# The last layer norm's second tile: two pieces of 256 columns for one of 512, and the piece in SBUF finished by GpSimd

## The chip, the cores and the metric

The kernel runs on one core of a Trainium2 chip. A core has TensorE (PE: matmuls, its weight loads shown apart as PEld), VectorE (DVE), ScalarE (ACT), GpSimd (POOL) and SyncE (SP, which only issues DMAs here). Data lies in SBUF and in PSUM, both of 128 partitions; matmuls write PSUM. The metric is the device time of one execution in microseconds, the median over the runs; lower is better.

## The reference

The program is a decoder trunk of two layers over 256 tokens of 1024 numbers, all in float32. A layer is a feed-forward half-step, a mixer (a gated spatial unit beside differential attention) and a second feed-forward half-step, each followed by a residual and a layer norm:

```
h = _swiglu(x, ffn_w1[l, 1], ffn_w3[l, 1], ffn_w2[l, 1])
x = _layernorm(ALPHA * x + 0.5 * h, ln_g[l, 2], ln_b[l, 2])
```

with `_layernorm(x, g, b) = (x - mean) * rsqrt(var + eps) * g + b`, mean and variance taken over the 1024 numbers of a token. The norm behind the second layer's second feed-forward is the last work of the program; its result is the output. The change lies in that norm.

## The kernel before, in words

Weights stream in from HBM, and each is split into a high and a low part in a faster matmul format; a product is three matmuls (high by high, low by high, high by low) that add up in PSUM. TensorE's order is the order in which the code is written. The other engines' order comes from a planner that sorts by priority and by dependences between regions of tiles; a wait is put in wherever an engine needs another's result. PSUM is given out as two groups of four banks, `bank()` and `side_bank()`, each handed out again when its last reader is done.

The 256 tokens are two tiles `t` of 128 (one token for each partition). The last feed-forward's second product, `gemm_seven`, makes 512 columns of the output at a time. Its last stretch goes over the second half of the output columns: for tile 0 all of 512:1024, then for tile 1 first 512:768 and then 768:1024 (line 410 is the matmul there and in the loops around it). Whenever a group of columns is done, `Norm.part` adds it to the residual in `y` (L625) and takes statistics of 256 columns each (L629). In tile 1 of the last norm, all columns below 768 are also multiplied at once by `g` (L631), since mean and variance of the row aren't known yet. So the work behind the last matmul concerns mostly the columns 768:1024 and the whole row's statistics.

`Norm.finish` then ends the tile. In the last norm:

- L636 (VectorE) joins the statistics to mean and variance, `mv`.
- L660 (GpSimd) adds eps to the variance, L661 (ScalarE) takes the square root; L674 to L676 (VectorE) make of these the factor `r` of each token, with one correction step.
- For tile 1 the pieces 512:768 and 0:512 of the row are taken through TensorE: an identity matmul (L666) copies `y * g` into PSUM, and a matmul with a diagonal matrix that holds minus the mean (made by ScalarE, L668) adds `-mean * g` to it (L670). A float32 matmul is two passes, each with its own weight load. The two pieces lie in two side banks.
- The third piece, 768:1024, stays in SBUF: L672 (VectorE) makes `(y - mean) * g` of it in one instruction.
- L678 (VectorE) multiplies each piece by `r` and adds `b`, in one scalar-tensor-tensor instruction; L679 stores it to HBM from the queues of SP and ScalarE (ACT) in turns. The pieces go in the order 768:1024 (SP), 512:768 (ACT), 0:512 (SP).

Tile 0 has the same three pieces, but all stay in SBUF and on VectorE; it ends while TensorE still works on tile 1.

Of the kernel before, what the change touches and what calls it, by code (L numbers as in the profile page):

```python
# [17 lines left out]
ALU = mybir.AluOpType  # L18
# [3 lines left out]
D = 1024  # L22
T = 256
NT = T // P
# [30 lines left out]
def trunk(ctx, tc, x, xT, w13a, w13b, w2, wb, wqk, wu, wg, wgr, wbr, wbrr, wo, gateb, gatebr, sgug, sgub, sguwT, sgubias, lam, diffg,  # L55
          lng, lnb, lngT, lnbT, cosT, sinT, out):
    nc = tc.nc
    V, A, G, PE = nc.vector, nc.scalar, nc.gpsimd, nc.tensor
# [22 lines left out]
    def side_bank():  # L81
        return psum.tile([P, 512], F32, tag="side", name=name("sbank"))
# [15 lines left out]
    def t512(s, n=3):  # L98
        return tmp.tile([P, 512], F32, tag="main", name=name(s), bufs=n)

    def s512(s, n=4):
        return tmp.tile([P, 512], F32, tag="side", name=name(s), bufs=n)

    def sm(s, n, dtype=F32, bufs=2):
        return small.tile([P, n], dtype, tag=f"{s}{n}", name=name(s), bufs=bufs)
# [31 lines left out]
    def beside(task, delay):  # L137
        tasks.append([clock[0] + delay, task])
# [16 lines left out]
    def behind(ins):  # L155

        return tc.issue_after(ins) if ins is not None else nullcontext()
# [93 lines left out]
    def rsqrt(v, eps):  # L251


        ve, y = sm("ve", 1), sm("yi", 1, I32)
        V.tensor_scalar(out=ve, in0=v, scalar1=eps, scalar2=None, op0=ALU.add)
        V.tensor_scalar(out=y, in0=ve.bitcast(I32), scalar1=-0.5, scalar2=RSQRT_START, op0=ALU.mult, op1=ALU.add)
        y = y.bitcast(F32)
        for e in (-26 / 27, -8 / 9, -2 / 3):
            a, z = sm("nwa", 1), sm("nwy", 1)
            V.tensor_scalar(out=a, in0=y, scalar1=y, scalar2=ve, op0=ALU.mult, op1=ALU.mult)  # L260
            V.tensor_scalar(out=z, in0=a, scalar1=3.0 * 2.0 ** e, scalar2=y, op0=ALU.subtract, op1=ALU.mult)
            y = z
        return y
# [321 lines left out]
    class Norm:  # L585
# [47 lines left out]
        def finish(self, t, waits):  # L633
            y = self.y[t]
            mv = sm("mv", 2)
            V.bn_aggr(out=mv, in_=self.st[t])  # L636
            if not self.last:
                r = rsqrt(mv[:, 1:2], self.eps)
                halves = slice(0, 512), slice(512, D)
                if t:  # L640
                    self.via += [t512("nvia") for _ in halves]
                for h in (0, 1) if t else (1, 0):
                    s = halves[h]
                    with behind(self.ends[t]):
                        self.ends[t] = V.tensor_scalar(out=y[:, s], in0=y[:, s], scalar1=mv[:, 0:1], scalar2=r,
                                                       op0=ALU.subtract, op1=ALU.mult).ins
                    if t:
                        self.ends[t] = self.plane(V, t, h, 1)
                if t == 0:
                    self.via.append(s512("nvia"))  # L650
                    for w in range(2):
                        self.ends[t] = self.plane(V, 0, 1, w)
                    beside(self.turned(waits), 0)
                else:
                    beside(self.sent(), 1.2)
                    beside(self.tokens(1), 10.8)
                return
            cuts = [slice(*c) for c in ((768, D), (512, 768), (0, 512))]
            ve, sd, r, a = (sm(n, 1) for n in ("ve", "nwy", "nwa", "nwy"))
            G.tensor_scalar(out=ve, in0=mv[:, 1:2], scalar1=self.eps, scalar2=None, op0=ALU.add)  # L660
            A.activation(sd, mv[:, 1:2], AF.Sqrt, bias=self.eps_t)  # L661
            rows = [y[:, s] for s in cuts]
            if t == NT - 1:
                rows[1:] = [side_bank()[:, : s.stop - s.start] for s in cuts[1:]]
                for b, s in zip(rows[1:], cuts[1:]):
                    PE.matmul(b, ident, y[:, s], start=True, stop=False)  # L666
                diag = self.minus[:, P : 2 * P]
                A.activation(diag, self.minus[:, :P], AF.Copy, scale=mv[:, 0:1])  # L668
                for b, s in zip(rows[1:], cuts[1:]):
                    PE.matmul(b, diag, self.g[:, s], start=False, stop=True)  # L670
            for s in cuts[: 1 if t == NT - 1 else 3]:
                V.scalar_tensor_tensor(out=y[:, s], in0=y[:, s], scalar=mv[:, 0:1], in1=self.g[:, s],  # L672
                                       op0=ALU.subtract, op1=ALU.mult)
            V.reciprocal(out=r, in_=sd)  # L674
            V.tensor_scalar(out=a, in0=r, scalar1=r, scalar2=ve, op0=ALU.mult, op1=ALU.mult)
            V.tensor_scalar(out=r, in0=a, scalar1=3.0, scalar2=r, op0=ALU.subtract, op1=ALU.mult)  # L676
            for n, (s, v) in enumerate(zip(cuts, rows)):
                V.scalar_tensor_tensor(out=y[:, s], in0=v, scalar=r, in1=self.b[:, s], op0=ALU.mult, op1=ALU.add)  # L678
                (nc.sync, A)[n % 2].dma_start(out[t * P : (t + 1) * P, s], y[:, s])  # L679

        def plane(self, eng, t, h, w):
# [653 lines left out]
```

## Time and profile before

| | |
|---|---|
| median of 3 runs | 1187.51 us (1187.22 to 1187.51) |
| profiled execution | 1188.13 us, span 1186.4 us |
| TensorE busy | 1180.8 us (100% of the span) |
| VectorE / ScalarE / GpSimd busy | 85% / 70% / 24% |
| GpSimd instructions | 352 |
| granted TensorE clock | 1.000 |

The span runs from the first to the last instruction of the core; the device time of the same execution has 1.7 us more around it. In the views, a row of the timeline is the start, the duration, engine, line, operation, output and inputs, shapes and the number of instructions merged into it; in brackets stands how long the engine was idle before and what ended that. A matmul's duration holds its way through the array, so that durations of matmuls in sequence overlap. Rows of one line give the durations' minimum, median and maximum.

### The profile page before, as it was taken

How to read it: one execution, taken by the hardware profiler on the slowest of the kernel's cores; microseconds unless marked ns; L12 is line 12 of the kernel's file. 1: busy time of each engine (PE TensorE's matmuls, PEld its weight loads, DVE VectorE, ACT ScalarE, POOL GpSimd, SP SyncE). 2: the span in 40 equal slices, each digit the busy share in tenths (PEclk: the TensorE clock that was granted, in tenths of full speed). 3: DMA queues.
4: the chain of work that ended last, by engine and by line, in shares of the span. 5: the costliest groups of instructions: out<-in, count | busy, mean ns of one | idle time of the engine just before them, and what ended most of it. 6: DMA issues, size and time to landing. Idle time of an engine off the chain costs nothing.

```text
span 1186.4 us, 16662 instructions
## 1 busy us (share of the span) xinstructions
PE 1180.8 (100%) x5771; PEld 994.4 (84%) x5771; DVE 1011.4 (85%) x1558; ACT 828.8 (70%) x1418; POOL 286.3 (24%) x352
## 2 busy tenths in 40 slices
PE   9999999999999999999999999999999999999998
PEld 8888888888888888888888888888888888888887
DVE  6989989788688989889899889888965989988895
ACT  6688658559955677886567876576788556679761
POOL 1011301247420220071020171004564112102300
PEclk9999999999999999999999999999999999999999
DMA  9868976768865658689668699586666755786881
GB/s 354 258 206 258 291 268 209 265 196 235 248 203 174 228 186 275 187 275 271 235 222 262 193 274 283 195 293 231 215 203 204 257 181 167 252 254 210 272 252 36
DMA packets 129476, 275.10 MB, mean 232 GB/s; under 512 B 89024, under 2 KB 90096, under 8 KB 105328
## 3 DMA queue, kind: packets, MB, share of 16 engines
q1 hardware_dynamic: 121968, 248.80, 63.1%
q0 software_dynamic: 6992, 24.71, 8.7%
q8 instruction: 45, 0.74, 0.2%
q10 hardware_dynamic: 432, 0.52, 0.1%
q14 instruction: 39, 0.32, 0.1%
HBM read 248.05 MB, written 1.05 MB: 210 GB/s over the span
## 4 chain that ended last, share of the span: by engine, by line
PE 99%; DMA 0%; DVE 0%; ACT 0%; issue 0%; ACTq 0%
PE bank L283 46%; PE bank L295 15%; PE sbank L376 12%; PE bank L410 10%; PE bank L302 8%; PE sbank L410 3%; PE bank L521 2%; PE sbank L994 1%; PE bank L376 1%; PE sbank L1050 1%; PE sbank L1168 1%; PE sbank L1048 0%; DMA xtok<-in_xT 0%; PE sbank L691 0%; PE sbank L670 0%; DVE xtok L678 0%
## 5 line engine op out<-in xcount | busy, mean ns | idle before, releaser
L197 DVE TENSOR_TENSOR wlo<-raw,whi 128x1024 fp32r<-128x1024 f32 (+1 forms) x346 | 378.7, 1121 | 53.1 <-ACT whi L195 39.2
L195 ACT ACTIVATE whi<-raw 128x1024 fp32r<-128x1024 f32 (+1 forms) x350 | 323.7, 952 | 136.5 <-PE bank L283 43.1
L283 PE MATMUL bank<-whi,x 128*128 128x512 f32 x1224 | 386.1, 390 | 0.0
L283 PEld LDWEIGHTS bank<-whi,x 128*128 128x128 f32 x1224 | 229.8, 188 | 47.5
L283 PE MATMUL bank<-wlo,x 128*128 128x512 f32 x612 | 238.2, 389 | 0.0
L249 DVE TENSOR_TENSOR wlo<-raw,whi 128x1024 fp32r<-128x1024 f32 (+1 forms) x124 | 143.7, 1182 | 18.1 <-ACT whi L247 9.4
L247 ACT ACTIVATE whi<-raw 128x1024 fp32r<-128x1024 f32 (+1 forms) x124 | 121.7, 1000 | 49.1 <-DVE raw L359 24.5
L295 PE MATMUL bank<-x,whi 128*128 128x512 f32 x640 | 153.3, 391 | 0.0
L295 PEld LDWEIGHTS bank<-x,whi 128*128 128x128 f32 x640 | 118.2, 188 | 23.8
L283 PEld LDWEIGHTS bank<-wlo,x 128*128 128x128 f32 x612 | 114.9, 188 | 23.4
L229 POOL COPY seven<-seven 128x512 uint16<-128x512 uint16 x16 | 58.1, 3690 | 134.4 <-DMA seven<-seven 74.0
L302 PEld LDWEIGHTS bank<-x,wlo 128*128 128x128 f32 x640 | 81.4, 191 | 2.9
L302 PE MATMUL bank<-x,wlo 128*128 128x256 f32 x640 | 82.6, 283 | 0.0
L410 PE MATMUL bank<-whi,hhi 128*128 128x512 f32 (+1 forms) x182 | 68.2, 374 | 0.0
L410 PE MATMUL bank<-whi,hlo 128*128 128x512 f32 (+1 forms) x182 | 67.9, 373 | 0.0
L410 PE MATMUL bank<-wlo,hhi 128*128 128x512 f32 (+1 forms) x182 | 67.9, 373 | 0.0
L970 POOL TENSOR_TENSOR swap<-swap,sin_t 128x512 f32<-128x512 f32 x16 | 27.8, 1737 | 101.2 <-DMA swap<-z 75.7
L734 POOL COPY nvia<-ntwo 128x256 uint16<-128x256 uint16 x20 | 9.9, 541 | 162.3 <-DMA ntwo<-nvia 150.0
L303 ACT ACTIVATE r<-bank 128x256 f32<-128x256 f32 x96 | 34.9, 372 | 16.5 <-PE bank L302 16.4
L376 PE MATMUL sbank<-whi,xhs 128*128 128x512 f32 x128 | 42.0, 389 | 0.0
L359 DVE TENSOR_TENSOR raw<-raw,home 128x1024 f32<-128x1024 f32 x32 | 38.5, 1217 | 1.2 <-DMA home<-in_w13b 1.2
L410 PEld LDWEIGHTS bank<-whi,hlo 128*128 128x128 f32 x182 | 34.3, 188 | 6.1
(283 smaller groups left out, 2148.7 us busy)
## 6 DMA issues: line engine op xcount, KB each, us to landing
raw<-in_w13b SPq DMA_DIRECT2D x68, 1024.0 KB, 5.8
raw<-in_w SPq DMA_DIRECT2D x32, 1024.0 KB, 6.9
raw<-in_wb SPq DMA_DIRECT2D x16, 1024.0 KB, 6.0
raw<-in_wqk SPq DMA_DIRECT2D x16, 1024.0 KB, 6.2
home<-in_w13b SPq DMA_DIRECT2D x16, 512.0 KB, 6.1
raw<-in_w13a SPq DMA_DIRECT2D x8, 1024.0 KB, 4.9
home<-in_w SPq DMA_DIRECT2D x16, 512.0 KB, 4.6
raw<-in_wgr SPq DMA_DIRECT2D x8, 1024.0 KB, 5.3
```

What stands on the lines that cost most here:

```text
L195: inline(A, A.activation(h, r, AF.Copy).ins)
L197: low = eng.tensor_tensor(out=w, in0=r, in1=h.bitcast(F32), op=ALU.subtract).ins
L229: eng.tensor_copy(out=o, in_=i)
L247: a = A.activation(hi, src, AF.Copy).ins
L249: return a, eng.tensor_tensor(out=lo, in0=src, in1=hi.bitcast(F32), op=ALU.subtract).ins
L283: PE.matmul(ps, xx, w, start=start and n == 0, stop=stop and n == 2)
L295: PE.matmul(b[-1], hi[:, k * P : (k + 1) * P], xc(k), start=k == 0, stop=False)
L302: PE.matmul(b[n][:, :T], lo[:, k * P : (k + 1) * P], xc(k)[:, :T], start=False, stop=k == KT - 1)
L303: emptied[0] = A.activation(r[:, s], b[n][:, T:], AF.Copy, scale=scale).ins
L359: inline(V, V.tensor_tensor(out=v, in0=v, in1=m, op=ALU.add).ins)
L376: PE.matmul(ps, x[o](k), y, start=start and k == n == 0, stop=stop and k == 3 and n == 2, skip_group_check=True)
L410: PE.matmul(q[c][t][:, :n] if o == 0 else more[:, :n], x(k, t), y, start=k == 8 and m == 0 and (c, t) != (1, 0), stop=k == FT - 1 and m == ...
```

## The change

For tile 1 of the last norm, and only there:

- The piece 0:512 is cut into 256:512 and 0:256. With 512:768 that makes three pieces of 256 columns in PSUM, in three side banks, with three identity and three diagonal matmuls instead of two each.
- The last step of the piece in SBUF (768:1024) goes from VectorE's one instruction to two on GpSimd: a multiply by `r` and an add of `b`, both in place.
- The order of the last step is now 512:768, 256:512, 0:256 (VectorE) and then 768:1024 (GpSimd). There are four stores instead of three, in turns on SP, ACT, SP, ACT.

Tile 0, the other norms and everything ahead of the last norm are written as before.

```
-            cuts = [slice(*c) for c in ((768, D), (512, 768), (0, 512))]
+            end = t == NT - 1
+            cuts = [slice(*c) for c in ((768, D), (512, 768), *(((256, 512), (0, 256)) if end else ((0, 512),)))]
             ve, sd, r, a = (sm(n, 1) for n in ("ve", "nwy", "nwa", "nwy"))
...
-            if t == NT - 1:
+            if end:
                 rows[1:] = [side_bank()[:, : s.stop - s.start] for s in cuts[1:]]
                 for b, s in zip(rows[1:], cuts[1:]):
                     PE.matmul(b, ident, y[:, s], start=True, stop=False)
...
-            for s in cuts[: 1 if t == NT - 1 else 3]:
+            for s in cuts[: 1 if end else 3]:
                 V.scalar_tensor_tensor(out=y[:, s], in0=y[:, s], scalar=mv[:, 0:1], in1=self.g[:, s],
                                        op0=ALU.subtract, op1=ALU.mult)
...
-            for n, (s, v) in enumerate(zip(cuts, rows)):
-                V.scalar_tensor_tensor(out=y[:, s], in0=v, scalar=r, in1=self.b[:, s], op0=ALU.mult, op1=ALU.add)
+            each = list(zip(cuts, rows))
+            for n, (s, v) in enumerate(each[1:] + each[:1] if end else each):
+                if end and s.stop == D:
+                    G.tensor_scalar(out=v, in0=v, scalar1=r, scalar2=None, op0=ALU.mult)
+                    G.tensor_tensor(out=v, in0=v, in1=self.b[:, s], op=ALU.add)
+                else:
+                    V.scalar_tensor_tensor(out=y[:, s], in0=v, scalar=r, in1=self.b[:, s], op0=ALU.mult, op1=ALU.add)
                 (nc.sync, A)[n % 2].dma_start(out[t * P : (t + 1) * P, s], y[:, s])
```

## The prediction

> **What bounds the kernel now.** I read the page first: the span, the busy shares and the chain that ended last.
>
> ```profile
> span 1186.4 us, 16662 instructions
> PE 1180.8 (100%) x5771; PEld 994.4 (84%) x5771; DVE 1011.4 (85%) x1558; ACT 828.8 (70%) x1418; POOL 286.3 (24%) x352
> PE 99%; DMA 0%; DVE 0%; ACT 0%; issue 0%; ACTq 0%
> ```
>
> TensorE carries 99% of the chain. The change touches nothing before the last norm, so only the tail behind the last matmuls of the feed-forward can move. That tail is the chain from the end of those matmuls (1179.16 us) to the end of the span, some 7.3 us, and I read it in order of time. From the chain of waits:
>
> ```profile
> 1180.10 0.27 DVE mv L636
> 1180.46 0.29 ACT nwy L661
> 1180.75 0.30 ACT minus L668
> 1181.10 1.57 PE sbank L670 x4
> 1182.69 0.75 DVE xtok L678
> ```
>
> Mean and variance go to ScalarE, which makes the diagonal matrix; TensorE adds the summand with the mean in four passes until 1182.67; VectorE then makes the last 512 columns. The timeline of VectorE and of the queues (start, duration) has the rest:
>
> ```profile
> 1181.40 0.22 DVE L676 TENSOR_SCALAR nwa<-nwy,nwa 128x1 f32<-128x1 f32 x1
> 1181.65 0.48 DVE L678 SCALAR_TENSOR_TENSOR xtok<-xtok,nwa,bc 128x256 f32<-128x256 f32 x1
> 1182.05 0.48 DVE L678 SCALAR_TENSOR_TENSOR xtok<-sbank,nwa,bc 128x256 f32<-128x256 f32 x1
> 1182.69 0.75 DVE L678 SCALAR_TENSOR_TENSOR xtok<-sbank,nwa,bc 128x512 f32<-128x512 f32 x1 [0.16 <-PE sbank L670]
> 1182.56 0.34 ACTq L679 DMA_DIRECT2D out_x<-xtok  x1
> 1183.47 0.33 SPq L679 DMA_DIRECT2D out_x<-xtok  x1
> ...
> out_x<-xtok SPq DMA_DIRECT2D x1, 256.0 KB, 2.0
> out_x<-xtok SPq DMA_DIRECT2D x1, 128.0 KB, 1.7
> out_x<-xtok ACTq DMA_DIRECT2D x1, 128.0 KB, 1.7
> ```
>
> The factor r is ready at 1181.62 (L676). The last piece is written at 1183.44, its store is issued at 1183.47 and lands 2.0 later, at 1185.47; what is left to 1186.4 is the program's closing and does not depend on the change. The last three rows are the DMA view's, with KB and us from issue to landing. So the end is set by: diagonal ready, TensorE's passes, one VectorE instruction of 0.75, one store of 2.0.
>
> **The change part by part.**
>
> *TensorE: two pieces become three.* Both the identity matmuls (L666) and the diagonal ones (L670) go from a 256 and a 512 to three of 256, each in two passes: four more passes in all, and as many weight loads.
>
> ```profile
> 1178.98 0.59 PE L666 MATMUL sbank<-xtok,ident 128*128 128x256 f32 x2
> 1179.41 1.02 PE L666 MATMUL sbank<-xtok,ident 128*128 128x512 f32 x2
> L666 PE MATMUL sbank<-xtok,ident 128*128 128x512 f32 x2 | 1.0, 593 | 0.0
> L666 PE MATMUL sbank<-xtok,ident 128*128 128x256 f32 x2 | 0.6, 378 | 0.0
> 1181.10 0.70 PE L670 MATMUL sbank<-bc,minus 128*128 128x256 f32 x2 [0.66 <-ACT minus L668]
> 1181.63 1.02 PE L670 MATMUL sbank<-bc,minus 128*128 128x512 f32 x2
> 1181.10 0.73 PEld L670 LDWEIGHTS sbank<-bc,minus 128*128 128x128 f32 x4 [1.49 <-ACT minus L668]
> ```
>
> Two 256-column passes span 0.59 with 0.378 each, so a pass starts 0.21 after the one before; for 512 columns it is 1.02 - 0.593 = 0.43, twice that. Cutting therefore costs no streaming, as long as the weight load (0.73 for four, below 0.19 each) fits into 0.21. The diagonal passes end for 512:768 at 1181.80 (1181.10 + 0.70), for 256:512 at 1181.80 + 0.42 = 1182.22, for 0:256 at 1182.65: the same end as before, 1182.67. Bound: the first two L670 passes stand 0.70 - 0.38 = 0.32 apart; at that spacing for the two added passes the end is 0.2 later. Below nothing there is no gain, since the columns are the same. I take zero, because L666's passes in sequence are the nearest rows. The identity passes are hidden in the 0.66 us in which TensorE waits for the diagonal; without that cover they too would cost at most 0.2.
>
> *The third PSUM bank.* The tag has four buffers; the norm takes the two not held by the second product and, now, one that this stage had used:
>
> ```profile
> 1169.11 0.69 DVE L625 SCALAR_TENSOR_TENSOR xtok<-xtok,sbank 128x512 f32<-128x512 f32 x1 [5.73 <-PE sbank L410]
> ```
>
> Its last reader ended at 1169.80, 9 us before L666, so the wait costs nothing. If the bank still were held, every later pass would stand behind it.
>
> *VectorE.* The SBUF piece leaves, so 512:768 is first. It can start at 1181.80 plus the 0.03 of a wait (r is there at 1181.65 already), and instructions in a row follow at 0.40 (1181.65 to 1182.05). 256:512 starts at about 1182.25, 0:256 at 1182.69 as before, when its passes are done; it takes 0.48 for 0.75 and ends at 1183.17. Gain 0.27. L672, which centres the SBUF piece, stays on VectorE.
>
> *GpSimd.* The piece 768:1024 gets two new instructions, a multiply by a column and an add of a 128x256 f32 tile. No row shows the first. Rows of one line, minimum/median/maximum ns:
>
> ```profile
> L249 POOL TENSOR_TENSOR x<-nvia,x x10: 732/737/752, 182.8 to 1006.9; 128x256 fp32r<-128x256 f32 x10
> L734 POOL COPY nvia<-ntwo x20: 470/480/1049, 179.5 to 1013.9; 128x256 uint16<-128x256 uint16 x20
> L275 POOL TENSOR_SCALAR nwa<-nwa x24: 220/224/1290, 270.6 to 915.3; 128x4 f32<-128x4 f32 x24
> L970 POOL TENSOR_TENSOR swap<-swap,sin_t x16: 1287/1703/2842, 216.2 to 845.0; 128x512 f32<-128x512 f32 x16
> 1180.45 0.21 POOL L660 TENSOR_SCALAR ve<-mv 128x1 f32<-128x1 f32 x1 [8.96 <-DVE mv L636]
> ```
>
> The add is L249's form: 0.74. The multiply lies between 0.22 (L275, four columns) and 0.74 (two inputs of that size); I take the one-input copy of 256 columns, 0.48. GpSimd started L660 0.08 after mv (1180.37), so here it starts at 1181.70, ends the multiply at 1182.18, the add, with 0.1 between, at 1183.02. With both at 0.74 it is 1183.28. The upper end is a stretched one: L970 went from 1.29 to 2.84, a factor of 2.2, which gives 1.06 + 0.1 + 1.63, until 1184.5. Nothing waits for GpSimd but this piece's store.
>
> Is it stretched? Two moments when GpSimd and VectorE worked together:
>
> ```profile
> 233.47 1.29 POOL L970 TENSOR_TENSOR swap<-swap,sin_t 128x512 f32<-128x512 f32 x1 [4.57 <-ACT pp L1008]
> 234.02 0.42 DVE L307 SCALAR_TENSOR_TENSOR z<-bank,r 128x256 f32<-128x256 f32 x1 [0.95 <-ACT r L303]
> 801.19 1.29 POOL L970 TENSOR_TENSOR swap<-swap,sin_t 128x512 f32<-128x512 f32 x1 [22.73 <-DMA swap<-z]
> 801.55 2.01 DVE L197 TENSOR_TENSOR wlo<-raw,whi 128x1024 fp32r<-128x1024 f32 x1
> ```
>
> Beside the scalar-tensor-tensor that reads PSUM and one SBUF tile both kept their undisturbed times (1.29, L970's minimum; 0.42). Beside the subtraction with two SBUF inputs VectorE paid instead: L197 took 2.01. The three L678 beside the new GpSimd work read PSUM and one SBUF tile, so I take no stretch. The Trainium skill, "SBUF — State Buffer", section "SBUF: two separate sides", says that GpSimd shares one port pair with VectorE under an exclusive lock, taken by a VectorE instruction with two SBUF inputs; by that rule the L678 from PSUM take no lock, and the two rows agree.
>
> The same skill's "GPSIMD Engine Reference", section "Engine selection", speaks against the change: it wants elementwise work on VectorE, GpSimd being about half as fast on two inputs. Weighed in this kernel: left on VectorE, the piece adds one slot of 0.40 and 0:256 starts at 1182.85, not 1182.69, so the rule costs 0.16 as long as GpSimd is not last; by the sum above it is not.
>
> *Queues.* Three stores become four, all of 128 KB. SP issues 512:768 (about 1182.35), then 0:256 at 1183.20; ACT's queue issues 256:512 at about 1182.78 (VectorE's end 1182.73, and 0.03), and behind it 768:1024, not before 0.38 later, at 1183.16; GpSimd's 1183.02 is hidden by that. So the last two stores go out within 0.05 of each other and share the DMA engines:
>
> ```profile
> 1182.95:1183.90 0.95, 0.00 (x0) 0.00 (x0) 0.49 (x1) 0.00 (x0) 0.00 (x0) 1.00 0.79 276
> 1184.30:1185.02 0.72, 0.00 (x0) 0.00 (x0) 0.00 (x0) 0.00 (x0) 0.00 (x0) 1.00 0.94 364
> ```
>
> These are two stretches of the span (length; last column GB/s): the two 128 KB stores together, and the 256 KB one. Alone, 128 KB lands in 1.7: 1183.20 + 1.7 = 1184.90, a gain of 0.57. Behind the other 128 KB at 364 GB/s, 0.36 later: 1185.26, a gain of 0.21. At 276 GB/s (0.47), with 0.1 for what is left of the 256:512 store: 1185.47, nothing. I take the middle, since the sharing is certain and the pieces' packets come back to back.
>
> *Sum.* VectorE -0.27, the smaller last store -0.30 (2.0 to 1.7), its neighbour +0.36: -0.21 us. The profiled execution took 1188.13 (span 1186.4 and 1.7 around it), so 1187.9 against it; it stands 0.6 above the median of the runs shown, 1187.51. Against the median: **1187.3 us**.
>
> **The rivals.**
>
> *No gain.* The stores overlap at 276 GB/s, or the added weight loads cost their 0.2: the end moves by less than 0.1 and the time is 1187.5. For it: the row with 276. Against: that stretch holds two stores issued 0.40 apart, with a dip between them.
>
> *GpSimd and VectorE block each other* (slower). If the L678 and the GpSimd instructions exclude each other, they go in turns from 1181.70: multiply to 1182.18, first L678 to 1182.66, add to 1183.40, two more L678 to 1184.36; the last store goes at 1184.39 and lands at 1186.09, +0.62 us, so 1188.1. Stretched by 2.2 instead, GpSimd ends at 1184.5 and its store lands at 1186.2, +0.8, so 1188.3. It decides from the point where GpSimd ends after about 1183.7 (1183.75 + 1.7 = 1185.45), some 2.0 us for the two instructions. For it: L970's maximum; against: the row at 233.47.
>
> *Slower by over 0.2%.* That is 2.4 us: GpSimd would have to end near 1186.1, 4.4 us after r. Only a multiply by a column that costs 3.6 us would do it. The costliest group of GpSimd has such a mean, but for copies of 512 columns that overlap work with two SBUF inputs:
>
> ```profile
> L229 POOL COPY seven<-seven 128x512 uint16<-128x512 uint16 x16 | 58.1, 3690 | 134.4 <-DMA seven<-seven 74.0
> ```
>
> **How the numbers follow.** A change of 0.2%, 2.4 us, is about what a measurement of this kernel can tell from no change. Chances: forecast 0.62, no gain 0.18, blocking 0.14, slower by over 0.2% 0.04, some effect that shortens by as much, which no row supports, 0.02. Only the last two leave the band: faster 0.02, same 0.94, slower 0.04. The likeliest case's own range is 1186.9 to 1187.8 (gain 0.57 to 0, and 0.3 of scatter, as among the runs shown). To hold 8 in 10 the range takes in the blocking and, below, the largest gain with the scatter doubled: 1186.5 to 1188.3.
>
> **What would show it.** Right: six L670 passes that end within 0.05 of 1.57 after the diagonal; three L678 from PSUM of 0.48, the last starting at the end of the passes; GpSimd with some 0.48 and 0.74, done before ACT's queue has issued 256:512; the last two stores within 0.1 of each other, landing about 0.2 earlier. Wrong: GpSimd's rows over 1 us, an L678 that starts late without TensorE as its releaser, L670 passes 0.3 apart, or a store of 768:1024 that lands last by more than 0.2. A time out of the range would mean that something before 1179 us moved, which I hold the change not to touch.

## The result and the profile after

The changed kernel takes 1190.2 us (median of 15 runs, 1189.76 to 1191.37), the kernel before 1187.51 (15 runs, 1187.21 to 1188.39): a ratio of 1.0022, with a 95% interval of 1.0015 to 1.0029. That is 2.7 us more, where the prediction had 0.2 less. In all that follows, differences in us are between medians; the ratios are taken over the single runs and so aren't exactly the quotients of the medians.

The head of the page of the changed kernel:

```profile
span 1188.4 us, 16675 instructions
PE 1179.7 (99%) x5775; PEld 994.4 (84%) x5775; DVE 1014.3 (85%) x1558; ACT 828.4 (70%) x1418; POOL 288.2 (24%) x354
```

The engines' busy times are those of before to within 3 us. That says little: over all the traces of this document GpSimd's busy time goes from 278 to 297 us. GpSimd has two more instructions. The tail's timeline (start, duration), from the first diagonal pass to the last stores:

```profile
1180.48 1.56 PE L671 MATMUL sbank<-bc,minus 128*128 128x256 f32 x6 [0.66 <-ACT minus L669]
1180.77 0.21 DVE L677 TENSOR_SCALAR nwa<-nwy,nwa 128x1 f32<-128x1 f32 x1
1181.09 0.95 POOL L681 TENSOR_SCALAR xtok<-xtok,nwa 128x256 f32<-128x256 f32 x1 [1.05 <-DVE nwa L677]
1181.21 1.35 DVE L684 SCALAR_TENSOR_TENSOR xtok<-sbank,nwa,bc 128x256 f32<-128x256 f32 x3 [0.23 <-PE sbank L671]
1181.72 1.20 SPq L685 DMA_DIRECT2D out_x<-xtok  x2
1182.12 0.72 POOL L682 TENSOR_TENSOR xtok<-xtok,bc 128x256 f32<-128x256 f32 x1
1182.88 0.85 ACTq L685 DMA_DIRECT2D out_x<-xtok  x2
```

(In this kernel L667 and L671 are the identity and diagonal matmuls, L681 and L682 GpSimd's two instructions, L684 and L685 VectorE's last step and the stores.) All stores are issued by 1183.7 and yet the span goes on to 1188.4. The chain of waits ends, other than before, on GpSimd's sequencer:

```profile
1181.09 0.95 POOL xtok L681
1182.04 0.04 issue
1182.08 0.77 POOLq L1337
```

L1337 is the end of the program (L1331 before): each engine's sequencer drains its engine, SP also waits for the stores (its first drain starts 0.1 to 0.2 us behind the last store's landing, but for the last kernel below), and then all meet. That line is asked for by itself here, the count of instructions first, then minimum/median/maximum ns, then the starts of the first and the last. The kernel before:

```profile
L1331 POOLq EVENT_SEMAPHORE  x4: 17/17/17, 1185.7 to 1186.3; - x4
L1331 POOLq DRAIN  x3: 46/93/4992, 1180.4 to 1186.2; - x3
L1331 SPq DRAIN  x3: 7/7/7, 1185.6 to 1185.9; - x3
```

And the changed one:

```profile
L1337 POOLq EVENT_SEMAPHORE  x4: 17/17/17, 1187.6 to 1188.3; - x4
L1337 POOLq DRAIN  x3: 46/102/5506, 1182.1 to 1188.1; - x3
L1337 SPq DRAIN  x3: 7/7/7, 1185.2 to 1187.8; - x3
```

The reader is to see GpSimd's first drain. Before, it starts at 1180.4, lasts 4.99 and ends at 1185.40, which is 4.74 after L660, GpSimd's last instruction, ended (1180.45 + 0.21). SP was through with the stores at 1185.6, so the drain was hidden, by 0.2 us. After, it starts at 1182.08, lasts 5.51 and ends at 1187.59: again 4.74 after GpSimd's last instruction (1182.12 + 0.72). SP was through at 1185.2 and waited, and the meeting (the first semaphore of GpSimd's) began at 1187.6 instead of 1185.7. Measured from the first diagonal pass (1181.10 before, 1180.48 after), GpSimd's last end moved from -0.44 to +2.37, the drain's end from 4.30 to 7.11, the meeting from 4.59 to 7.15: 2.56 us, of the 2.7 that the runs show.

### The profile page after: what moved, and what is told of

Same layout as the page of the kernel before. It is cut to its first block, busy times and chain, and to the rows that moved or that the text cites. A ratio compares the mean times of both kernels' runs of the same rounds, so it can differ in the third digit from the quotient of the medians.

```text
span 1188.4 us, 16675 instructions
## 1 busy us (share of the span) xinstructions
PE 1179.7 (99%) x5775; PEld 994.4 (84%) x5775; DVE 1014.3 (85%) x1558; ACT 828.4 (70%) x1418; POOL 288.2 (24%) x354
## 4 chain that ended last, share of the span: by engine, by line
PE 99%; DMA 0%; issue 0%; POOL 0%; DVE 0%; ACT 0%; POOLq 0%
PE bank L283 46%; PE bank L295 15%; PE sbank L376 12%; PE bank L410 10%; PE bank L302 8%; PE sbank L410 3%; PE bank L521 2%; PE sbank L1000 1%; PE bank L376 1%; PE sbank L1056 1%; PE sbank L1174 1%; PE sbank L1054 0%; DMA xtok<-in_xT 0%; PE sbank L697 0%; POOL xtok L681 0%
## 5 line engine op out<-in xcount | busy, mean ns | idle before, releaser
L410 PEld LDWEIGHTS bank<-whi,hhi 128*128 128x128 f32 x182 | 34.3, 188 | 6.0
```

What stands on the lines that cost most here:

```text
L410: PE.matmul(q[c][t][:, :n] if o == 0 else more[:, :n], x(k, t), y, start=k == 8 and m == 0 and (c, t) != (1, 0), stop=k == FT - 1 and m == ...
```

## The experiments

My theory after the traces: the program can't close until GpSimd has drained, 4.74 us after its last instruction, and the change put that instruction behind the factor r. Two rivals: the cut itself costs (more passes, a third bank, four stores), or GpSimd's piece is late and its store with it.

The first four kernels take these apart. **The cut alone**, all last steps on VectorE:

```
-            for n, (s, v) in enumerate(each[1:] + each[:1] if end else each):
-                if end and s.stop == D:
-                    G.tensor_scalar(out=v, in0=v, scalar1=r, scalar2=None, op0=ALU.mult)
-                    G.tensor_tensor(out=v, in0=v, in1=self.b[:, s], op=ALU.add)
-                else:
-                    V.scalar_tensor_tensor(out=y[:, s], in0=v, scalar=r, in1=self.b[:, s], op0=ALU.mult, op1=ALU.add)
+            for n, (s, v) in enumerate(each):
+                V.scalar_tensor_tensor(out=y[:, s], in0=v, scalar=r, in1=self.b[:, s], op0=ALU.mult, op1=ALU.add)
```

> The change without its GpSimd part: three pieces of 256 in PSUM, four stores, and all four last steps on VectorE, 768:1024 first. Theory 'GpSimd's closing drain' (the program closes only 4.74 us after GpSimd's last instruction, which the change moved from 1180.66 to the end of its add): GpSimd's last instruction is L660 again, its drain ends near 1185.4 as before, so the loss is gone and the time is between -0.2 and +0.1 us of before. Rival 'the cut' (more passes, a third bank, four stores): most of the +2.7 us stays. Rival 'the late piece' (the store of GpSimd's piece and the store queued with it): loss gone as well, between -0.3 and +0.1 us.

Measured 1187.16 us beside 1187.34 for the kernel before: -0.18, ratio 0.9996 (0.9987 to 1.0006). The cut costs nothing, so that rival falls.

**GpSimd's piece alone**, without the cut:

```
-            cuts = [slice(*c) for c in ((768, D), (512, 768), *(((256, 512), (0, 256)) if end else ((0, 512),)))]
+            cuts = [slice(*c) for c in ((768, D), (512, 768), (0, 512))]
```

> The other part alone: 0:512 stays one piece, 768:1024 gets its factor and summand from GpSimd. Drain theory: GpSimd ends 1.86 us after r as in the changed kernel, the drain 4.74 us later, 2.8 us later than before: +2.4 to +2.7 us. Rival 'the cut': 0, within 0.2 us. Rival 'the late piece': at most +0.3 us, since the stores of the changed kernel landed only about 0.3 us later than before (measured from the first diagonal pass).

Measured 1189.88, +2.54, ratio 1.0021 (1.0012 to 1.0030). The loss is in GpSimd's part. Its drain:

```profile
L1337 POOLq DRAIN  x3: 46/93/5509, 1181.9 to 1187.9; - x3
```

It ends at 1187.42, again 4.74 behind GpSimd's last instruction (1182.68).

**One column behind the factor**, the kernel before with a GpSimd instruction that no other work needs:

```
+            if t == NT - 1:
+                G.tensor_scalar(out=sm("nwa", 1), in0=r, scalar1=1.0, scalar2=None, op0=ALU.mult)
             for n, (s, v) in enumerate(zip(cuts, rows)):
```

> The kernel before, and one added GpSimd instruction of one column that reads r and writes a scratch column nobody reads; no piece, no store and no matmul is changed. Drain theory: GpSimd's last instruction ends 0.3 us after r instead of 0.96 before it, the drain ends near 1186.7 instead of 1185.4, which passes the stores' end (1185.6): +0.8 to +1.2 us. Rivals 'the late piece' and 'the cut': 0, within 0.2 us.

Measured 1188.6, +1.26, ratio 1.0008 (0.9999 to 1.0018). By the interval alone that is just not told from nothing; the trace has its cause. VectorE's and GpSimd's rows in the timeline, and then GpSimd's drain in the closing line:

```profile
1180.72 0.48 DVE L680 SCALAR_TENSOR_TENSOR xtok<-xtok,nwa,bc 128x256 f32<-128x256 f32 x1
1180.77 0.52 POOL L678 TENSOR_SCALAR nwa<-nwa 128x1 f32<-128x1 f32 x1 [0.72 <-DVE nwa L676]
```

```profile
L1333 POOLq DRAIN  x3: 46/93/5301, 1180.7 to 1186.5; - x3
```

The instruction ends at 1181.29, the drain at 1186.03, 4.74 later, with the stores through 4.50 after the first diagonal pass as before (4.49). It is slightly above what I expected since this one column took 0.52 us, not 0.22. L680 here is VectorE's last step on the piece in SBUF, with two inputs in SBUF; it ends at 1181.21, and GpSimd's column 0.08 behind it.

**One column behind the last piece**, the same instruction after VectorE's last:

```
                 (nc.sync, A)[n % 2].dma_start(out[t * P : (t + 1) * P, s], y[:, s])
+            if t == NT - 1:
+                G.tensor_scalar(out=sm("nwa", 1), in0=y[:, :1], scalar1=1.0, scalar2=None, op0=ALU.mult)
```

> The kernel before, and one added GpSimd instruction of one column that reads a column of the last piece that VectorE writes, into scratch. Drain theory: GpSimd ends near 1183.75, the drain near 1188.5: +2.6 to +3.0 us, that is 1.8 us more than with the instruction behind r. Rivals: 0, within 0.2 us. If the added time is the same as with the instruction behind r, it is a fixed price of any added instruction and not the place of the last one.

Measured 1190.45, +3.11, ratio 1.0024 (1.0014 to 1.0033), 1.85 us more than with the instruction behind r (1.56 by the traces, see the table below). So it isn't a price of the added instruction but of where the last one stands. The same two views:

```profile
1183.39 0.23 POOL L681 TENSOR_SCALAR nwa<-xtok 128x1 f32<-128x1 f32 x1 [2.87 <-DVE xtok L678]
```

```profile
L1333 POOLq DRAIN  x3: 46/102/5007, 1183.4 to 1188.9; - x3
```

1183.62 to 1188.36: 4.74. An instruction of 0.23 us that computes nothing anyone reads put the meeting off further than the whole change did (7.44 us after the first diagonal pass, against 7.15); the intervals of the two times overlap.

The next four ask what follows from it. **Eps on VectorE**, the kernel before without GpSimd in the tail:

```
-            G.tensor_scalar(out=ve, in0=mv[:, 1:2], scalar1=self.eps, scalar2=None, op0=ALU.add)
+            V.tensor_scalar(out=ve, in0=mv[:, 1:2], scalar1=self.eps, scalar2=None, op0=ALU.add)
```

> The kernel before with eps added by VectorE instead of GpSimd (both tiles of the last norm), so that GpSimd does nothing in the tail. Drain theory: the drain still ends 4.74 us after GpSimd's last instruction, which is now tens of us earlier, and is done long before the stores; the stores alone set the closing, and they did already before (4.59 us after the first diagonal pass, the drain at 4.30): within 0.15 us of before. If the drain waits for the end of the other engines or for the stores, it ends in the tail all the same and has another length than 4.74.

Measured 1187.58 beside 1187.57, ratio 1.0 (0.9991 to 1.0009). As the stores were the later of the two, nothing is won by taking the drain away. The drain now runs while TensorE still multiplies. It isn't one of 4.74 us, as I had expected, but of 13.5; GpSimd's last work is now a DMA that it issues (see the last section).

**The cut and eps on VectorE**, both edits together, GpSimd idle in the tail:

> The cut of 0:512 with all last steps on VectorE, and eps added by VectorE. With the cut alone the stores were ready 4.14 us after the first diagonal pass but the drain ended at 4.30 and the closing began at 4.35. Drain theory: without GpSimd in the tail the closing begins at 4.1 to 4.2 us, 0.4 to 0.5 us earlier than in the kernel before: -0.3 to -0.5 us, 0.15 to 0.3 us below the cut alone. If only the stores set the closing in both, it is the same as the cut alone (-0.18).

Measured 1187.02, the kernel before 1187.57: -0.55, ratio 0.9997 (0.9988 to 1.0006). The interval can't tell it from no change; the traces show what moved. For the cut alone, then for both:

```profile
L1333 POOLq EVENT_SEMAPHORE  x4: 17/17/17, 1184.6 to 1185.2; - x4
L1333 POOLq DRAIN  x3: 46/93/4992, 1179.5 to 1185.0; - x3
L1333 SPq DRAIN  x3: 7/7/7, 1184.3 to 1184.8; - x3
```

```profile
L1333 POOLq EVENT_SEMAPHORE  x4: 17/17/17, 1184.4 to 1185.1; - x4
L1333 POOLq DRAIN  x3: 46/93/11850, 1135.7 to 1184.9; - x3
L1333 SPq DRAIN  x3: 7/7/7, 1184.3 to 1184.6; - x3
```

With the cut alone SP is through at 1184.27 and the meeting comes 0.31 later, at 1184.58, when the drain behind L661 (the addition of eps in that kernel) has ended (1184.54). With both, GpSimd's drain was over some 37 us earlier and the meeting comes 0.10 after SP. Of all kernels run this one has the earliest meeting in its trace and the lowest median; its time isn't told apart from that of the cut alone.

**Other queues**, the changed kernel with 512:768 and 768:1024 stored from ScalarE's queue and the other two from SP's:

```
-                (nc.sync, A)[n % 2].dma_start(out[t * P : (t + 1) * P, s], y[:, s])
+                ((A, nc.sync, nc.sync, A) if end else (nc.sync, A, nc.sync))[n].dma_start(out[t * P : (t + 1) * P, s], y[:, s])
```

> The changed kernel with 256:512 and 0:256 stored from SP and 512:768 from ScalarE's queue, so that 256:512 no longer stands behind the store of GpSimd's piece. Drain theory: the stores land 0.2 to 0.5 us earlier against the first diagonal pass, and the time does not change, +2.4 to +2.8 us on before. Rival 'the late piece': the time falls with the stores by 0.2 to 0.5 us.

Measured 1190.11, +2.54, ratio 1.0021 (1.0012 to 1.0030). The stores were through 4.41 after the first diagonal pass instead of 4.76, and the time stayed (the meeting at 7.14 instead of 7.15). So the rival of the late piece falls too: its store is late, but not what the end waits for.

**Prices on GpSimd**, five instructions behind VectorE's last one:

```
+            if t == NT - 1:
+                w = s512("late")[:, :256]
+                G.tensor_scalar(out=w, in0=y[:, :256], scalar1=r, scalar2=None, op0=ALU.mult)
+                G.tensor_tensor(out=w, in0=w, in1=self.b[:, :256], op=ALU.add)
+                G.tensor_scalar(out=w, in0=w, scalar1=0.5, scalar2=None, op0=ALU.mult)
+                G.tensor_scalar(out=w, in0=w, scalar1=r, scalar2=None, op0=ALU.mult)
+                G.tensor_copy(out=w, in_=self.g[:, :256])
```

> The kernel before with five GpSimd instructions of 128x256 f32 behind VectorE's last one, when VectorE is idle, into scratch: multiply by the column r, add of a tile, multiply by a number, multiply by the column r again, copy. If the change's multiply was slow because VectorE worked beside it, the multiply by a column takes about 0.5 us here; if it is its own price, about 0.95 us, and the multiply by a number tells whether the column makes it so. Drain theory: 4.74 us from the end of the fifth to the end of the drain, and about 4.2 us more than the kernel with one tiny instruction at this place, less the tiny one's 0.2: +6 to +7 us on before.

One run, 1194.69, +7.1. The timeline of GpSimd, VectorE being idle from 1183.15 on, and then the drain:

```profile
1183.25 0.95 POOL L682 TENSOR_SCALAR late<-xtok,nwa 128x256 f32<-128x256 f32 x1 [2.59 <-DVE xtok L678]
1184.29 0.72 POOL L683 TENSOR_TENSOR late<-late,bc 128x256 f32<-128x256 f32 x1
1185.10 0.87 POOL L684 TENSOR_SCALAR late<-late 128x256 f32<-128x256 f32 x1
1186.07 0.93 POOL L685 TENSOR_SCALAR late<-late,nwa 128x256 f32<-128x256 f32 x1
1187.06 0.40 POOL L686 COPY late<-bc 128x256 f32<-128x256 f32 x1
```

```profile
L1338 POOLq DRAIN  x3: 46/102/5159, 1187.0 to 1192.7; - x3
```

The multiply takes its 0.95 with VectorE idle as it did beside VectorE, and 0.87 with a plain number: a price of its own, not a collision. The drain again ends 4.74 after the last (1187.45 to 1192.19).

All kernels in one table. The middle columns are us from the first diagonal pass, worked out from each trace; "stores" is the start of SP's first drain.

| kernel | GpSimd's last end | drain's end | stores | meeting | meeting against before | time against before |
|---|---|---|---|---|---|---|
| before | -0.44 | 4.30 | 4.49 | 4.59 | | |
| the change | 2.37 | 7.11 | 4.76 | 7.15 | +2.56 | +2.69 |
| cut alone | -0.44 | 4.30 | 4.04 | 4.35 | -0.24 | -0.18 |
| GpSimd's piece alone | 2.38 | 7.12 | 4.92 | 7.16 | +2.57 | +2.54 |
| one column behind r | 1.09 | 5.84 | 4.50 | 5.88 | +1.29 | +1.26 |
| one column behind the last piece | 2.66 | 7.40 | 4.50 | 7.44 | +2.85 | +3.11 |
| eps on VectorE | tail empty | early | 4.50 | 4.60 | +0.01 | +0.01 |
| cut, eps on VectorE | tail empty | early | 4.00 | 4.09 | -0.50 | -0.55 |
| other queues | 2.36 | 7.10 | 4.41 | 7.14 | +2.55 | +2.54 |
| five prices | 6.65 | 11.39 | | 11.44 | +6.85 | +7.1 |

The meeting comes 0.05 us after GpSimd's drain or 0.1 after the stores are through, whichever is later, in every row; and the time follows it within 0.3 us. The times of three kernels (one column behind r, one behind the last piece, five prices) lie by up to 0.12 us above the range that I had expected, that of the cut with eps on VectorE 0.05 below its own. In the last row SP's first drain started at 6.68, 0.03 after GpSimd's last instruction and long after the last store had landed (4.36), so no time of the stores stands there.

## Why the prediction was wrong

**The step that failed** is one clause: "what is left to 1186.4 is the program's closing and does not depend on the change". The 0.93 us behind the last landing were treated as a constant. But the closing begins with the later of two things, the stores and GpSimd's drain, and in the kernel before these ended within 0.2 us of each other. The companion of the error is "Nothing waits for GpSimd but this piece's store": the program's end waits for it as well. The first profile's line L1331 had the row (4992 ns, from 1180.4); I followed the chain of waits, which in that profile ended on VectorE's last instruction, and didn't ask for the closing line. The sum had no term for the drain: the meeting came 2.56 us later, of which the stores alone would have made 0.27 and the drain makes the other 2.29. The last sign in the prediction misled too: a time out of the range was to mean that something before 1179 us had moved, and here those 2.56 of the 2.7 us lie behind the first diagonal pass.

**TensorE: right.** Six passes took 1.56, as four had by the timeline (1.57 by the chain of waits); the added weight loads hid.

**The third bank: right.** The six passes wait for the diagonal alone (0.66, as before).

**VectorE: right.** From the first diagonal pass to its last end it took 2.08 us (1180.48 to 1182.56); the forecast was 2.07 (1181.10 to 1183.17), against 2.34 before.

**GpSimd: mis-sized.** The add took 0.72 for 0.74. The multiply took 0.95 for 0.48: the copy of two-byte numbers was the wrong neighbour, and the upper bound, the two-input add at 0.74, was no bound. Of the 0.45 by which GpSimd ended later than forecast (2.37 after the first diagonal pass for 1183.02 - 1181.10 = 1.92) nearly all is this, and with the drain behind it that went into the time. The Trainium skill's "GPSIMD Engine Reference", section "Engine selection", puts one-input work on GpSimd at roughly line rate and two-input work at half of VectorE's speed; the two multiplies with one tile as input differ from that, 0.95 and 0.87 against 0.72 for the add of two tiles, and the measurement decides; the copy, also of one tile, took 0.40.

**Queues: wrong order.** I put 256:512 ahead of 768:1024 on ScalarE's queue. Both of its stores went out at 1182.88 and later, right behind GpSimd's end (1182.84), though VectorE had ended 256:512 at about 1182.13; the first is GpSimd's piece (it waits for GpSimd's semaphore, the second for VectorE's), which the planner had put ahead. The stores were through 0.27 later than before, where I had -0.21. With the queues set by hand, they came 0.08 earlier than before. Neither moved the time.

**The rivals.** That GpSimd and VectorE block each other did not happen: the three L684 took what L678 had (0.48, the last number a mean in ns).

```profile
L684 DVE SCALAR_TENSOR_TENSOR xtok<-sbank,nwa,bc 128x256 f32<-128x256 f32 x3 | 1.3, 484 | 0.2 <-PE sbank L671 0.2
```

These three read PSUM and one SBUF tile. Beside an instruction of VectorE with two inputs in SBUF it may be otherwise: the one column behind r took 0.52 beside L680, and the one behind the last piece 0.23 with VectorE idle. They suggest that there GpSimd is held, where the prediction's rows had VectorE pay; no run was made to show it.

That GpSimd decides only if it ends "after about 1183.7" was far off: with the drain it decides from 1185.59 - 4.74 = 1180.85 on, before r is even known, so any GpSimd work behind r had to lose. The loss over 0.2% had a chance of 0.04 because its only mechanism asked for a multiply of 3.6 us. The advice to keep elementwise work on VectorE, whose price I had put at 0.16 us, does cost VectorE about that: its last end came 2.21 after the first diagonal pass with the cut alone, 2.08 in the changed kernel. It turned out right for another reason, GpSimd's drain; and with all four last steps on VectorE the stores came earlier than in any kernel in which GpSimd made a piece.

What the traces don't settle is what GpSimd does in those 4.74 us.

## What to carry to other kernels

The end of a program is a meeting of all engines, and an engine that looks idle in the tail can still be the last to come: look at the closing line's drains, not only at the chain of waits, and note how long behind its last instruction each engine's drain ends. On this core GpSimd's last instruction has to lie some 4.7 us ahead of where the other engines are through; in the last microseconds a one-column instruction on it cost 1.3 to 3.1 us, and 256 columns left on VectorE put off VectorE's end by 0.13. And a cover of 0.2 us is no cover: a saving elsewhere in the tail (the cut) uncovered the same drain from the other side.

## What the runs showed of the hardware that I had not expected

- GpSimd's closing drain ended 4.74 us after the end of its last instruction in all eight traces with such an instruction in the tail, whether that was an add of 256 columns or of one, a multiply of one column or a copy. The Trainium skill's "VectorE: DVE Perf Modes", section "The DRAIN you can't avoid", has the drains that the runtime puts around a kernel at about 12 ns on all five engines. The drains here stand at a line of the kernel itself, so they may not be those: SP's took 7 ns each, GpSimd's first one 5 us.
- Where the last GpSimd work was a DMA that it issued (eps on VectorE), the drain lasted longer. The DMA and the drain with eps on VectorE, then the DMA with the cut as well (the drain's row stands above):

```profile
raw<-in_w POOLq DMA_DIRECT2D x1, 512.0 KB, 11.1
L1331 POOLq DRAIN  x3: 46/102/13512, 1135.9 to 1185.6; - x3
...
raw<-in_w POOLq DMA_DIRECT2D x1, 512.0 KB, 9.5
```

Issued at 1135.90, that DMA landed at 1147.01, and the drain ended at 1149.39; with the cut as well it landed at 1145.16, and the drain ended at 1147.54. So it ended 2.38 us behind the landing both times, though the drains differ by 1.7 us. That it waits for the landing is what two cases suggest, not more.
- A multiply of 128x256 f32 by a column or a number took GpSimd longer (0.95, 0.87) than an add of two tiles of the same size (0.72), and a copy 0.40.
